# Rotary tables moved from VectorE to GpSimd, with a new order of TensorE's steps, in a hybrid decoder layer

## The chip, the cores and the metric

The kernel runs on one core of a Trainium2 chip. The metric is the device time of one execution in microseconds. The engines are called PE (TensorE), DVE (VectorE), ACT (ScalarE), POOL (GpSimd) and SP (SyncE, which issues most transfers). Times inside a profile are microseconds from the first instruction of the span.

## What is computed

One decoder layer over 256 positions of width 1024, in float32: an input projection, two groups of eight heads (A: dilated windows with a position bias, B: low-rank latents with a rotary part), an output projection with a residual, and a feed-forward block of width 4096 with squared ReLU. Cut to what matters:

```
xn = rms_norm(x, norm_mix_g)
qa, ka, va, c_q, c_kv, k_rope = split(xn @ w_in)      # 512, 512, 512, 768, 256, 32 columns
qa, ka = rms_norm per head of 64;  out_a = dilated_attention(qa, ka, va, rel_bias)
qb = rms_norm(c_q) @ w_uq;  k_nope, vb = split(rms_norm(c_kv) @ w_ukv)
qb, kb = rms_norm per head of 96 (64 plain, 32 rotary)
qb[..., 64:], kb[..., 64:] = apply_rope(..., positions)
out_b = causal softmax attention(qb, kb, vb)
h = x + concat(out_a, out_b) @ w_o
h = h + relu(rms_norm(h) @ w_ff1)^2 @ w_ff2

def apply_rope(x, positions):                 # r = 32
    ang = positions * inv_freq                # (256, 16)
    x1, x2 = x[..., :16], x[..., 16:]
    return concat([x1 * cos(ang) - x2 * sin(ang), x2 * cos(ang) + x1 * sin(ang)])
```

## The kernel before

**Tiling.** The 256 positions are two tiles of 128 partitions (`t` = 0, 1). Weights come in chunks of up to 1 MB (`raw`, three buffers, issued on SP) and are split piece by piece, 1024 columns at most, into two parts that a matmul takes exactly: ACT casts the upper part (`his`, line 243), DVE subtracts it from the weight (`los`, line 244). Each has five buffers. A step of a projection (`three`) is six matmuls: upper weights with upper and lower activations, lower weights with upper activations. Activations are split in the same way (line 276, `two`): first the columns of x, later the latents after their transposition.

**Order.** TensorE's order is written out by hand: the string `STEPS` (line 125) is read from left to right, a star gives repetitions, and every matmul is kept in that order until the feed-forward block. In it `p` is a step of q's and k's projection of group A, `b` the spread position bias, `c0`, `c1` steps of the query latents, `l` of the key latents, `g` of A's values; `A0`, `A1` transpose A's q and k; `L0` to `L2` transpose and split the latents; `x0` to `x5` are A's scores with softmax, and `y0` to `y5` the transposes of these probabilities (`keys_first`); `q0`, `q1`, `k0`, `k1` project B's queries and keys, `Q` and `K` turn them (transposes, then copies by ACT and DVE, line 636), `a` is A's probabilities times values, `s`, `t`, `v` are the same three for B, `w` steps of the output projection, `h` the residual. `r0` calls `rotary_tables()` and issues nothing on TensorE. What the other engines run is ordered by a scheduler, which fills their queues from a model of the times; each engine then works its queue off strictly in order.

**Rotary tables.** Lines 352 to 389 reduce the angle and evaluate a polynomial for sine and cosine, all on DVE, in instructions over 128x32 or 128x64 (tiles `ang`, `arg`, `sq`, `trig`); `rotary_tables()` (line 392) multiplies them by gains into `tabc` and `tabs`. The keys' tables are first read in `have_ckv` (line 588) by POOL, the queries' in `have_q` (line 646) by DVE.

**Norms of A's heads.** `normed_heads` (line 473) squares q's and k's projection on ACT, sums per head on DVE (line 454), takes the power -1/2 on POOL (lines 478 and 266, tile `s_a`, four of them: q's two tiles, then k's two), and DVE multiplies (line 481). The softmax of `probs` (line 519) is a minimum over scores on DVE (line 528), the exponential on ACT (531), and a multiplication by the reciprocal sum on DVE (534), which `keys_first` waits for.

Of the kernel before, what the change touches and what calls it, by code (L numbers as in the profile page):

```python
# [30 lines left out]
NOPE, ROPE = 64, 32  # L31
# [16 lines left out]
HR = ROPE // 2  # L48
MAGIC = 12582912.0
# [61 lines left out]
for _i, (_, _b, _n) in enumerate(CHUNKS):  # L111
# [10 lines left out]

STEPS = """p*13 b0 p*3 c0*4 A0 c0*4 r0 c1*5 A1 c1*3 l*2 L0 l*3 x0 l*2 x1 l g y0 g L1 g x2 g y1 g x3 g y2 g L2 g x4 k0 y3
    k0 x5 q0*2 y4 q0*4 k1*2 y5 q1 Q0 q1*2 K0 q1 a0 a1 q1*2 K1 s0 w s1 w*2 Q1 s2 w t0 s3 w t1 s4 t2 s5 w t3 v0 t4 w*2
    t5 w v1 w*5 h0 w*2 h1"""

WO_STEPS = [(k, b) for b in range(2) for k in range(4)]
WO_STEPS += [(4, 0), (5, 0), (4, 1), (6, 0), (7, 0), (5, 1), (6, 1), (7, 1)]  # L130
# [14 lines left out]
TWO_PI = pieces(2 * math.pi, 12, 2)
SIN = [(-1.0) ** i / math.factorial(2 * i + 1) for i in range(7)]
# [20 lines left out]
def tile_layer(ctx, tc, x, xt, cols_in, rows_in, w_all, out):  # L167
    nc = tc.nc
    V, A, G, T = nc.vector, nc.scalar, nc.gpsimd, Products(tc)

    const = ctx.enter_context(tc.tile_pool(name="const", bufs=1))
# [16 lines left out]
    def bank(pool=mm):  # L188
        return pool.tile([P, 512], F32, name=pool.name)
# [4 lines left out]
    def tiny(n, name, bufs=1):  # L194
        return small.tile([P, n], F32, name=name, bufs=bufs)
# [152 lines left out]
    load(out=rows, in_=rows_in)  # L348
    starting.clear()


    ang = [const.tile([P, NT, HR], F32, name=f"ang{i}") for i in range(4)]
    pos = const.tile([P, NT], F32, name="pos")
    V.tensor_copy(out=pos, in_=first[:, F_POS:F_POS + NT].bitcast(I32))
    a0, kh, kl, r = ang
    full = [P, NT, HR]
    inv = first[:, F_INV:F_INV + HR]
    V.tensor_tensor(out=a0, in0=pos.unsqueeze(2).broadcast_to(full), in1=inv.unsqueeze(1).broadcast_to(full), op=ALU.mult)

    def turns(out, in_, period):  # L360
        V.tensor_scalar(out=out, in0=in_, scalar1=1.0 / period, scalar2=MAGIC, op0=ALU.mult, op1=ALU.add)
        V.tensor_scalar(out=out, in0=out, scalar1=MAGIC, scalar2=None, op0=ALU.subtract)

    def less(out, in_, k, part):
        V.scalar_tensor_tensor(out=out, in0=k, scalar=-part, in1=in_, op0=ALU.mult, op1=ALU.add)

    turns(kh, a0, 2 * math.pi * 4096)
    for part in TWO_PI_HI[:3]:
        less(a0, a0, kh, part)
    less(r, a0, kh, TWO_PI_HI[3])  # L370
    turns(kl, r, 2 * math.pi)
    for k, part in ((kl, TWO_PI[0]), (kh, TWO_PI_HI[3]), (kl, TWO_PI[1]), (kh, TWO_PI_HI[4]), (kl, TWO_PI[2]), (kh, TWO_PI_HI[5])):
        less(a0, a0, k, part)
    arg = const.tile([P, NT, 2, HR], F32, name="arg")
    V.scalar_tensor_tensor(out=r, in0=a0, scalar=-1.0, in1=a0, op0=ALU.mult, op1=ALU.max)
    V.tensor_scalar(out=arg[:, :, 0, :], in0=r, scalar1=-1.0, scalar2=math.pi / 2, op0=ALU.mult, op1=ALU.add)
    V.tensor_scalar(out=r, in0=a0, scalar1=-1.0, scalar2=math.pi, op0=ALU.mult, op1=ALU.add)
    V.tensor_tensor(out=a0, in0=a0, in1=r, op=ALU.min)
    V.tensor_scalar(out=r, in0=a0, scalar1=-1.0, scalar2=-math.pi, op0=ALU.mult, op1=ALU.add)
    V.tensor_tensor(out=arg[:, :, 1, :], in0=a0, in1=r, op=ALU.max)  # L380
    af = arg.rearrange("p t c f -> p (t c f)")
    sq = const.tile([P, NT * ROPE], F32, name="sq")
    trig = const.tile([P, NT, 2, HR], F32, name="trig")
    tf = trig.rearrange("p t c f -> p (t c f)")
    V.tensor_tensor(out=sq, in0=af, in1=af, op=ALU.mult)
    V.tensor_scalar(out=tf, in0=sq, scalar1=SIN[6], scalar2=None, op0=ALU.mult)
    for c in SIN[5:0:-1]:
        V.scalar_tensor_tensor(out=tf, in0=tf, scalar=c, in1=sq, op0=ALU.add, op1=ALU.mult)
    V.scalar_tensor_tensor(out=tf, in0=tf, scalar=1.0, in1=af, op0=ALU.add, op1=ALU.mult)
    tabs = []  # L390

    def rotary_tables():
        for i in range(2):
            tab_c = const.tile([P, NT, ROPE], F32, name=f"tabc{i}")
            tab_s = const.tile([P, NT, ROPE], F32, name=f"tabs{i}")
            g1, g2 = (cols[:, C_ROPE + i * ROPE + z * HR:C_ROPE + i * ROPE + (z + 1) * HR].unsqueeze(1).broadcast_to(full) for z in range(2))
            cos, sin = trig[:, :, 0, :], trig[:, :, 1, :]
            V.tensor_tensor(out=tab_c[:, :, 0:HR], in0=cos, in1=g1, op=ALU.mult)
            V.tensor_tensor(out=tab_c[:, :, HR:], in0=cos, in1=g2, op=ALU.mult)
            V.scalar_tensor_tensor(out=tab_s[:, :, 0:HR], in0=sin, scalar=-1.0, in1=g2, op0=ALU.mult, op1=ALU.mult)  # L400
            V.tensor_tensor(out=tab_s[:, :, HR:], in0=sin, in1=g1, op=ALU.mult)
            tabs.append((tab_c, tab_s))

    def sumsq(src, dst):
        junk = sqs.tile([P, DM], mybir.dt.bfloat16, name="sqs")
        return A.activation(out=junk[:, :src.shape[1]], in_=src, func=AF.Square, accum_out=dst)  # L406
# [294 lines left out]
    for b in range(2):  # L701
# [2 lines left out]
        runs[f"k{b}"] = project_steps(f"ukv{b}", cT, KQ, KKV, lambda ps, b=b: have_kv(b, ps))  # L704
    single = {
        "A": stack_heads,
        "b": lambda i: spread_bias(),
        "r": lambda i: rotary_tables(),
        "x": begin_a,
        "y": lambda i: keys_first(UNITS[i], sb_a.pop(i), pT_a[UNITS[i][0]]),  # L710
        "L": lambda i: transposed_split([c[:, 384 * i:] for c in cn], 3 * i, 3 if i < 2 else KKV, G_C, *cT[:2]),
# [146 lines left out]
```

## Time and profile before

| | us |
|---|---|
| median of 3 runs | 322.23 (321.21 to 322.47) |
| the profiled execution | 322.39, its span 320.6 |
| PE busy | 310.5 (97%) |
| DVE busy | 219.9 (69%) |
| ACT busy | 178.4 (56%) |
| POOL busy | 40.9 (13%) |

A busy time counts the instructions of an engine in the span. A line in the profile names the source line, the engine, the operation, the tile that it writes and the tiles that it reads; `[2.00 <-DVE half L534]` says that the engine stood idle for 2.00 us before it and was released by DVE's instruction of line 534. Where a row has `x2`, two instructions of a kind are put together. The granted clock (PEclk) is TensorE's, 1.00 being 2.4 GHz.

### The profile page before, as it was taken

How to read it: one execution, taken by the hardware profiler on the slowest of the kernel's cores; microseconds unless marked ns; L12 is line 12 of the kernel's file. 1: busy time of each engine (PE TensorE's matmuls, PEld its weight loads, DVE VectorE, ACT ScalarE, POOL GpSimd, SP SyncE). 2: the span in 40 equal slices, each digit the busy share in tenths (PEclk: the TensorE clock that was granted, in tenths of full speed). 3: DMA queues.
4: the chain of work that ended last, by engine and by line, in shares of the span. 5: the costliest groups of instructions: out<-in, count | busy, mean ns of one | idle time of the engine just before them, and what ended most of it. 6: DMA issues, size and time to landing. Idle time of an engine off the chain costs nothing.

```text
span 320.6 us, 4529 instructions
## 1 busy us (share of the span) xinstructions
PE 310.5 (97%) x1646; PEld 264.9 (83%) x1646; DVE 219.9 (69%) x421; ACT 178.4 (56%) x317; POOL 40.9 (13%) x66
## 2 busy tenths in 40 slices
PE   8999999799989899999999999999999999999995
PEld 6778999587988687888888888888888888888883
DVE  3998999757868985538995584674754945845722
ACT  4885678567775684419575354543643643635400
POOL 3057501700381200000200000000000000000000
PEclk9999999799999999999999999999999999999999
DMA  7996883434342453304658455645556374553002
GB/s 226 406 372 236 288 306 140 116 101 147 133 164 66 117 214 131 133 0 138 257 193 308 164 186 200 214 181 184 212 151 241 133 234 159 190 203 131 0 35 98
DMA packets 12326, 56.95 MB, mean 178 GB/s; under 512 B 1384, under 2 KB 3440, under 8 KB 7696
## 3 DMA queue, kind: packets, MB, share of 16 engines
q1 hardware_dynamic: 10560, 54.94, 49.3%
q10 hardware_dynamic: 1744, 1.73, 1.9%
q8 instruction: 13, 0.21, 0.3%
q14 instruction: 9, 0.07, 0.1%
HBM read 55.07 MB, written 1.06 MB: 175 GB/s over the span
## 4 chain that ended last, share of the span: by engine, by line
PE 86%; DVE 7%; ACT 3%; DMA 1%; issue 1%; DVEq 0%; ACTq 0%
PE acc L160 48%; PE sc L160 20%; PE mm L160 15%; PE mm L163 4%; DVE los L244 3%; ACT his L243 2%; DMA raw<-in_weights_dram 1%; DVE half L528 1%; ACT sqs L406 1%; DVE s_q L454 0%; DVE two L276 0%; DVE half L767 0%; ACT two L275 0%; DVE nats L620 0%; ACT big L642 0%
## 5 line engine op out<-in xcount | busy, mean ns | idle before, releaser
L244 DVE TENSOR_TENSOR los<-raw,his 128x1024 fp32r<-128x1024 f32 (+3 forms) x106 | 120.9, 1148 | 61.4 <-ACT his L243 60.2
L243 ACT CAST his<-raw 128x1024 fp32r<-128x1024 f32 (+3 forms) x106 | 104.1, 990 | 87.5 <-PE acc L160 48.8
L160 PE MATMUL acc<-his,two 128*128 128x512 f32 (+2 forms) x288 | 73.9, 378 | 0.8 <-DVE two L276 0.5
L160 PE MATMUL acc<-two,his 128*128 128x512 f32 x240 | 63.1, 393 | 0.2 <-DVE half L767 0.2
L160 PEld LDWEIGHTS acc<-his,two 128*128 128x128 f32 x288 | 50.6, 190 | 8.3 <-issue 1.0
L160 PE MATMUL mm<-his,big 128*128 128x512 f32 x128 | 49.1, 390 | 0.0
L160 PE MATMUL sc<-his,big 128*128 128x512 f32 x128 | 49.0, 389 | 0.0
L160 PEld LDWEIGHTS acc<-two,his 128*128 128x128 f32 x240 | 42.6, 189 | 7.6 <-DVE half L767 0.4
L160 PE MATMUL acc<-los,two 128*128 128x512 f32 (+2 forms) x144 | 41.5, 369 | 0.0
L160 PEld LDWEIGHTS acc<-two,los 128*128 128x128 f32 x240 | 34.5, 190 | 3.4
L160 PE MATMUL acc<-two,los 128*128 128x256 f32 x240 | 35.8, 282 | 0.0
L160 PEld LDWEIGHTS acc<-los,two 128*128 128x128 f32 x144 | 26.5, 190 | 4.2 <-DVE los L244 0.6
L160 PEld LDWEIGHTS mm<-his,big 128*128 128x128 f32 x128 | 24.1, 188 | 4.8
L160 PEld LDWEIGHTS sc<-his,big 128*128 128x128 f32 x128 | 24.1, 188 | 4.8
L160 PE MATMUL sc<-los,big 128*128 128x512 f32 x64 | 24.9, 389 | 0.0
L160 PE MATMUL mm<-los,big 128*128 128x512 f32 x64 | 24.9, 389 | 0.0
L531 ACT ACTIVATE half<-half,mx 128x128 f32<-128x128 f32 (+1 forms) x32 | 14.3, 451 | 6.5 <-DVE mx L528 6.5
L766 ACT COPY half<-acc 128x256 f32<-128x256 f32 x30 | 9.8, 374 | 7.8 <-PE acc L160 7.8
L160 PEld LDWEIGHTS mm<-los,big 128*128 128x128 f32 x64 | 12.0, 188 | 2.5
L160 PEld LDWEIGHTS sc<-los,big 128*128 128x128 f32 x64 | 12.0, 188 | 2.5
L767 DVE TENSOR_TENSOR half<-acc,half 128x256 f32<-128x256 f32 x30 | 11.4, 418 | 1.3 <-ACT half L766 1.3
L770 ACT CAST big<-half 128x512 fp32r<-128x512 f32 x16 | 10.0, 625 | 3.9 <-DVE half L768 3.9
(146 smaller groups left out, 305.2 us busy)
## 6 DMA issues: line engine op xcount, KB each, us to landing
raw<-in_weights_dram SPq DMA_DIRECT2D x36, 1024.0 KB, 4.8
raw<-in_weights_dram SPq DMA_DIRECT2D x13, 512.0 KB, 5.3
raw<-in_weights_dram SPq DMA_DIRECT2D x6, 768.0 KB, 4.3
raw<-in_weights_dram SPq DMA_DIRECT2D x2, 576.0 KB, 4.6
x<-in_x_dram SPq DMA_DIRECT2D x2, 512.0 KB, 8.6
big<-vec_d ACTq DMA_DIRECT2D x1, 1024.0 KB, 6.7
big<-in_xt_dram SPq DMA_DIRECT2D x3, 256.0 KB, 6.9
raw<-in_weights_dram SPq DMA_DIRECT2D x2, 384.0 KB, 2.9
```

The costliest lines, as they stand in the source:

```text
L160: return self._issue(self.tc.nc.tensor.matmul(**kw))
L163: return self._issue(self.tc.nc.tensor.transpose(**kw))
L243: pinned(A.copy(out=hi, in_=raw))
L244: pinned(V.tensor_tensor(out=lo, in0=raw, in1=hi.bitcast(F32), op=ALU.subtract))
L406: return A.activation(out=junk[:, :src.shape[1]], in_=src, func=AF.Square, accum_out=dst)
L528: V.tensor_tensor_reduce(out=sb[:, i, :], in0=ps[:, i, :], in1=mask(h)[:, S - nk:], op0=ALU.add, op1=ALU.min, scale=scale(t, h), scalar=-L ...
L531: A.activation(out=sb[:, i, :], in_=sb[:, i, :], func=AF.Exp, scale=-1.0, bias=mx[:, i:i + 1], accum_out=mx[:, 4 + i:5 + i])
L766: A.copy(out=zs, in_=ps[2 * b + i][:, S:])
L767: V.tensor_tensor(out=zs, in0=ps[2 * b + i][:, 0:S], in1=zs, op=ALU.add)
L770: A.copy(out=ht[:, sl, :], in_=s3)
```

## The change

`rotary_tables()` now holds the whole computation, and nearly all of it is written for POOL (`G`). Where DVE had one instruction for two operations (`scalar_tensor_tensor`), POOL gets two (`two_step`), with a scratch tile `rot2` of two buffers. The cast of `pos` and three steps with a maximum or minimum stay on DVE. `r0` is called behind `A1`, no longer in front of `c1`. In `STEPS`, `L1` and `L2` stand earlier, `g` steps move between the `x` and `y`, `Q0` behind `a1`, and one `w` moves from behind `t4` to the front of `s0`.

```diff
-STEPS = """p*13 b0 p*3 c0*4 A0 c0*4 r0 c1*5 A1 c1*3 l*2 L0 l*3 x0 l*2 x1 l g y0 g L1 g x2 g y1 g x3 g y2 g L2 g x4 k0 y3
-    k0 x5 q0*2 y4 q0*4 k1*2 y5 q1 Q0 q1*2 K0 q1 a0 a1 q1*2 K1 s0 w s1 w*2 Q1 s2 w t0 s3 w t1 s4 t2 s5 w t3 v0 t4 w*2
-    t5 w v1 w*5 h0 w*2 h1"""
+STEPS = """p*13 b0 p*3 c0*4 A0 c0*4 c1*5 A1 r0 c1*3 l*2 L0 l*3 x0 l*2 L1 l x1 g*2 y0 x2 g*2 y1 g L2 x3 g*2 y2 g x4 k0 y3 k0 x5
+    q0*2 y4 q0*4 k1*2 y5 q1*3 K0 q1 a0 a1 Q0 q1*2 K1 w s0 w s1 w*2 Q1 s2 w t0 s3 w t1 s4 t2 s5 w t3 v0 t4 w t5 w v1 w*5
+    h0 w*2 h1"""
...
-    V.tensor_tensor(out=a0, in0=pos.unsqueeze(2).broadcast_to(full), in1=inv.unsqueeze(1).broadcast_to(full), op=ALU.mult)
...
-    def less(out, in_, k, part):
-        V.scalar_tensor_tensor(out=out, in0=k, scalar=-part, in1=in_, op0=ALU.mult, op1=ALU.add)
...
+    def rotary_tables():
...
+        V.tensor_copy(out=pos, in_=first[:, F_POS:F_POS + NT].bitcast(I32))
...
+        G.tensor_tensor(out=a0, in0=pos.unsqueeze(2).broadcast_to(full), in1=inv.unsqueeze(1).broadcast_to(full), op=ALU.mult)
+
+        def two_step(out, in0, scalar, in1, op0, op1):
+            tmp = tiny(NT * ROPE, "rot2", bufs=2)[:, :math.prod(in0.shape[1:])]
+            tmp = tmp.rearrange("p (t f) -> p t f", t=NT) if len(in0.shape) == 3 else tmp
+            G.tensor_scalar(out=tmp, in0=in0, scalar1=scalar, scalar2=None, op0=op0)
+            G.tensor_tensor(out=out, in0=tmp, in1=in1, op=op1)
+
+        def turns(out, in_, period):
+            G.tensor_scalar(out=out, in0=in_, scalar1=1.0 / period, scalar2=MAGIC, op0=ALU.mult, op1=ALU.add)
+            G.tensor_scalar(out=out, in0=out, scalar1=MAGIC, scalar2=None, op0=ALU.subtract)
+
+        def less(out, in_, k, part):
+            two_step(out=out, in0=k, scalar=-part, in1=in_, op0=ALU.mult, op1=ALU.add)
...
+        V.scalar_tensor_tensor(out=r, in0=a0, scalar=-1.0, in1=a0, op0=ALU.mult, op1=ALU.max)
+        G.tensor_scalar(out=arg[:, :, 0, :], in0=r, scalar1=-1.0, scalar2=math.pi / 2, op0=ALU.mult, op1=ALU.add)
+        G.tensor_scalar(out=r, in0=a0, scalar1=-1.0, scalar2=math.pi, op0=ALU.mult, op1=ALU.add)
+        V.tensor_tensor(out=a0, in0=a0, in1=r, op=ALU.min)
+        G.tensor_scalar(out=r, in0=a0, scalar1=-1.0, scalar2=-math.pi, op0=ALU.mult, op1=ALU.add)
+        V.tensor_tensor(out=arg[:, :, 1, :], in0=a0, in1=r, op=ALU.max)
...
+        for c in SIN[5:0:-1]:
+            two_step(out=tf, in0=tf, scalar=c, in1=sq, op0=ALU.add, op1=ALU.mult)
```

How it moves the queues is shown at three places. The names are those of the code, with a buffer's number where rows would read alike; a star of TensorE's steps is not printed. In the changed kernel the lines behind the tables have numbers higher by 6 (244, 266 and 276 stay).

DVE's queue at the splits of q's and k's weights, before:

```order
L276 SCALAR_TENSOR_TENSOR two<-big,first,two 128x256 x2
L365 SCALAR_TENSOR_TENSOR ang_198<-ang_199,ang_198 128x32
L244 TENSOR_TENSOR los<-raw,his 128x1024
L375 SCALAR_TENSOR_TENSOR ang_201<-ang_198 128x32
L276 SCALAR_TENSOR_TENSOR two<-big,first,two 128x256
L376 TENSOR_SCALAR arg<-ang_201 128x2x16
L244 TENSOR_TENSOR los<-raw,his 128x1024
```

and after:

```order
L276 SCALAR_TENSOR_TENSOR two<-big,first,two 128x256 x2
L398 SCALAR_TENSOR_TENSOR ang_565<-ang_562 128x32
L244 TENSOR_TENSOR los<-raw,his 128x1024
L276 SCALAR_TENSOR_TENSOR two<-big,first,two 128x256
L401 TENSOR_TENSOR ang_562<-ang_562,ang_565 128x32
L244 TENSOR_TENSOR los<-raw,his 128x1024
L403 TENSOR_TENSOR arg<-ang_562,ang_565 128x2x16
```

The rotary steps that fed each other on DVE are gone, and the three that are left read tiles that POOL writes.

POOL's queue at the norms of A's heads, before (`s_a` of q's two tiles, then of k's first):

```order
L478 TENSOR_SCALAR s_a_361<-s_a_361,eps_x 128x8
L266 TENSOR_TENSOR s_a_361<-s_a_361,mhalf 128x8
L478 TENSOR_SCALAR s_a_369<-s_a_369,eps_x 128x8
L266 TENSOR_TENSOR s_a_369<-s_a_369,mhalf 128x8
L478 TENSOR_SCALAR s_a_422<-s_a_422,eps_x 128x8
L266 TENSOR_TENSOR s_a_422<-s_a_422,mhalf 128x8
```

and after, from q's second tile to k's first (twelve steps of the tables stand at the line of dots):

```order
L484 TENSOR_SCALAR s_a_331<-s_a_331,eps_x 128x8
L380 TENSOR_SCALAR rot_626<-trig 128x64
L266 TENSOR_TENSOR s_a_331<-s_a_331,mhalf 128x8
L381 TENSOR_TENSOR trig<-rot_626,sq 128x64
...
L484 TENSOR_SCALAR s_a_384<-s_a_384,eps_x 128x8
L381 TENSOR_TENSOR tabs_641<-rot_644,cols 128x2x16
L266 TENSOR_TENSOR s_a_384<-s_a_384,mhalf 128x8
```

Fifty instructions of the tables now stand ahead of the power for k's first tile, and in the same queue as it.

TensorE's order around the first transposes of probabilities (`mm<-ident,half`), before:

```order
L160 MATMUL sc<-big,two 128x256 x4
L160 MATMUL acc<-his,two 128x288 x4
L160 MATMUL acc<-los,two 128x288 x2
L160 MATMUL acc<-his,two 128x512 x4
L160 MATMUL acc<-los,two 128x512 x2
L163 MATMUL mm<-ident,half 128x128 x4
```

and after:

```order
L163 MATMUL mm<-ident,nats 128x128 x6
L160 MATMUL acc<-his,two 128x288 x4
L160 MATMUL acc<-los,two 128x288 x2
L160 MATMUL sc<-big,two 128x256 x4
L160 MATMUL acc<-his,two 128x512 x4
L160 MATMUL acc<-los,two 128x512 x2
L160 MATMUL acc<-his,two 128x512 x4
L160 MATMUL acc<-los,two 128x512 x2
L163 MATMUL mm<-ident,half 128x128 x4
```

The six transposes of the latents (`mm<-ident,nats`) and a second step of the values (`acc`, 128x512) now come before the probabilities' transposes.

## Rows read from the trace of the kernel before

**Rows 1.** The page, busy times of the engines in the whole span

```profile
PE 310.5 (97%) x1646; PEld 264.9 (83%) x1646; DVE 219.9 (69%) x421; ACT 178.4 (56%) x317; POOL 40.9 (13%) x66
```

**Rows 2.** Waits of PE: us in total, times, longest

```profile
PE mm L163 <- DVE half L534: 2.0, 1, 2.0
PE mm L163 <- DVE nats L621: 1.3, 2, 1.0
...
PE mm L163 <- ACT big L642: 0.8, 1, 0.8
PE acc L160 <- DVE two L276: 0.5, 1, 0.5
```

**Rows 3.** Windows: length, busy time of each engine, then the granted clock

```profile
5.50:57.00 51.50, 51.50 (x282) 45.61 (x282) 48.30 (x109) 38.76 (x69) 16.51 (x20) 1.00 0.81 290
60.00:64.00 4.00, 4.00 (x17) 3.19 (x17) 2.11 (x4) 1.67 (x3) 3.64 (x12) 0.69 0.29 117
88.00:92.00 4.00, 2.96 (x20) 2.43 (x19) 4.00 (x14) 3.87 (x10) 2.44 (x3) 1.00 0.55 211
```

**Rows 4.** Timeline of POOL: start, us, instruction; last, a window as in rows 3

```profile
26.61 3.60 POOL L266 TENSOR_TENSOR s_a<-s_a,mhalf 128x8 f32<-128x8 f32 x1
...
33.49 1.64 POOL L266 TENSOR_TENSOR s_a<-s_a,mhalf 128x8 f32<-128x8 f32 x1
...
89.78 1.98 POOL L653 TENSOR_SCALAR s_q<-s_q,eps_q 128x4 f32<-128x4 f32 x1 [0.43 <-DVE s_q L454]
...
58.76:61.21 2.45, 2.15 (x7) 1.87 (x8) 2.07 (x8) 0.45 (x4) 2.12 (x10) 0.57 0.59 132
```

**Rows 5.** Timeline of DVE beside the first and the last of these

```profile
26.91 1.80 DVE L244 TENSOR_TENSOR los<-raw,his 128x768 fp32r<-128x768 f32 x2
30.25 0.69 DVE L481 TENSOR_TENSOR half<-acc,s_a 128x512 f32<-128x512 f32 x1 [1.54 <-POOL s_a L266]
...
90.00 1.21 DVE L244 TENSOR_TENSOR los<-raw,his 128x1024 fp32r<-128x1024 f32 x1
91.14 0.48 DVE L621 TENSOR_TENSOR nats<-nats,rot 128x128 f32<-128x128 f32 x2
```

**Rows 6.** Timeline of DVE, the cast of the positions and the split at 15 us

```profile
5.26 0.16 DVE L354 CAST pos<-first 128x2 f32<-128x2 int32 x1
...
15.15 1.22 DVE L244 TENSOR_TENSOR los<-raw,his 128x1024 fp32r<-128x1024 f32 x1
```

**Rows 7.** Timeline of PE, the first matmuls with the lower part of that split

```profile
17.77 0.62 PE L160 MATMUL acc<-los,two 128*128 128x512 f32 x2
```

**Rows 8.** Windows of line 244, then of line 276: length, DVE busy, count

```profile
5.00:35.50 30.50, 16.41 (x17) 1.00 0.91 339
...
5.00:35.50 30.50, 3.67 (x8) 1.00 0.91 339
```

**Rows 9.** DVE from the third `s_a` to the first probabilities: timeline, then the window

```profile
35.51 0.68 DVE L481 TENSOR_TENSOR half<-acc,s_a 128x512 f32<-128x512 f32 x1
...
58.63 0.87 DVE L534 TENSOR_SCALAR half<-half,mx 128x128 f32<-128x128 f32 x4
...
35.50:58.60 23.10, 21.56 (x143) 20.94 (x142) 22.06 (x45) 18.48 (x44) 4.64 (x9) 1.00 0.67 223
```

**Rows 10.** Timeline of PE: L1's transposes and a step of `g`, with their followers

```profile
62.49 0.82 PE L163 MATMUL mm<-ident,nats 128*128 128x128 f32 x6
63.08 1.17 PE L160 MATMUL acc<-his,two 128*128 128x512 f32 x4
...
65.00 1.09 PE L160 MATMUL acc<-his,two 128*128 128x512 f32 x4
...
66.40 0.60 PE L163 MATMUL mm<-ident,half 128*128 128x128 f32 x4
```

**Rows 11.** Timelines of DVE and of PE at t5, B's last probabilities

```profile
122.82 0.61 DVE L534 TENSOR_SCALAR half<-half,mx 128x256 f32<-128x256 f32 x2
...
124.73 0.60 PE L163 MATMUL mm<-ident,half 128*128 128x128 f32 x4
```

More of the change, by code (lines that the diff above doesn't have):

```diff
@@ L349, in tile_layer @@
     starting.clear()
[L352 to L357, printed above, removed]
-    V.tensor_tensor(out=a0, in0=pos.unsqueeze(2).broadcast_to(full), in1=inv.unsqueeze(1).broadcast_to(full), op=ALU.mult)
-    def turns(out, in_, period):
-        V.tensor_scalar(out=out, in0=in_, scalar1=1.0 / period, scalar2=MAGIC, op0=ALU.mult, op1=ALU.add)
-        V.tensor_scalar(out=out, in0=out, scalar1=MAGIC, scalar2=None, op0=ALU.subtract)
@@ L364, in less @@
-    def less(out, in_, k, part):
-        V.scalar_tensor_tensor(out=out, in0=k, scalar=-part, in1=in_, op0=ALU.mult, op1=ALU.add)
[L367 to L402, printed above, removed]
@@ L416, in tile_layer @@
     G.tensor_scalar(out=eps_x, in0=ssx, scalar1=EPS, scalar2=None, op0=ALU.mult)
+    tabs = []
+    def rotary_tables():
+        ang = [const.tile([P, NT, HR], F32, name=f"ang{i}") for i in range(4)]
+        pos = const.tile([P, NT], F32, name="pos")
+        V.tensor_copy(out=pos, in_=first[:, F_POS:F_POS + NT].bitcast(I32))
+        a0, kh, kl, r = ang
+        full = [P, NT, HR]
+        inv = first[:, F_INV:F_INV + HR]
+        G.tensor_tensor(out=a0, in0=pos.unsqueeze(2).broadcast_to(full), in1=inv.unsqueeze(1).broadcast_to(full), op=ALU.mult)
[9 more added lines that the diff above has]
+            two_step(out=out, in0=k, scalar=-part, in1=in_, op0=ALU.mult, op1=ALU.add)
+        turns(kh, a0, 2 * math.pi * 4096)
+        for part in TWO_PI_HI[:3]:
+            less(a0, a0, kh, part)
+        less(r, a0, kh, TWO_PI_HI[3])
+        turns(kl, r, 2 * math.pi)
+        for k, part in ((kl, TWO_PI[0]), (kh, TWO_PI_HI[3]), (kl, TWO_PI[1]), (kh, TWO_PI_HI[4]), (kl, TWO_PI[2]), (kh, TWO_PI_HI[5])):
+            less(a0, a0, k, part)
+        arg = const.tile([P, NT, 2, HR], F32, name="arg")
+        V.scalar_tensor_tensor(out=r, in0=a0, scalar=-1.0, in1=a0, op0=ALU.mult, op1=ALU.max)
[4 more added lines that the diff above has]
+        V.tensor_tensor(out=arg[:, :, 1, :], in0=a0, in1=r, op=ALU.max)
+        af = arg.rearrange("p t c f -> p (t c f)")
+        sq = const.tile([P, NT * ROPE], F32, name="sq")
+        trig = const.tile([P, NT, 2, HR], F32, name="trig")
+        tf = trig.rearrange("p t c f -> p (t c f)")
+        G.tensor_tensor(out=sq, in0=af, in1=af, op=ALU.mult)
+        G.tensor_scalar(out=tf, in0=sq, scalar1=SIN[6], scalar2=None, op0=ALU.mult)
+        for c in SIN[5:0:-1]:
+            two_step(out=tf, in0=tf, scalar=c, in1=sq, op0=ALU.add, op1=ALU.mult)
+        two_step(out=tf, in0=tf, scalar=1.0, in1=af, op0=ALU.add, op1=ALU.mult)
+        for i in range(2):
+            tab_c = const.tile([P, NT, ROPE], F32, name=f"tabc{i}")
+            tab_s = const.tile([P, NT, ROPE], F32, name=f"tabs{i}")
+            g1, g2 = (cols[:, C_ROPE + i * ROPE + z * HR:C_ROPE + i * ROPE + (z + 1) * HR].unsqueeze(1).broadcast_to(full) for z in range(2))
+            cos, sin = trig[:, :, 0, :], trig[:, :, 1, :]
+            G.tensor_tensor(out=tab_c[:, :, 0:HR], in0=cos, in1=g1, op=ALU.mult)
+            G.tensor_tensor(out=tab_c[:, :, HR:], in0=cos, in1=g2, op=ALU.mult)
+            two_step(out=tab_s[:, :, 0:HR], in0=sin, scalar=-1.0, in1=g2, op0=ALU.mult, op1=ALU.mult)
+            G.tensor_tensor(out=tab_s[:, :, HR:], in0=sin, in1=g1, op=ALU.mult)
+            tabs.append((tab_c, tab_s))
@@ L706, in tile_layer @@
         "A": stack_heads,
+        "r": lambda i: rotary_tables(),
         "b": lambda i: spread_bias(),
-        "r": lambda i: rotary_tables(),
         "x": begin_a,
```

## The prediction

> **What bounds the kernel now.** I read the busy shares first: TensorE works for 310.5 of the 320.6 us of the profiled span [rows 1], so any gain has to come out of time in which it stands still or runs slowly. Next I read who TensorE waits for [rows 2]: DVE's probabilities once for 2.0 us, DVE's turned q (`nats`) for 1.3 us in two waits, ScalarE's copy of turned q for 0.8, a split of the turned latents for 0.5. That is 4.6 us, and these are the places that the new order rearranges. Then the clock: in the stretch 60 to 64 us, behind the 2.0 us wait, the granted clock was 0.69, a mix of the two levels 2.4 and 1.2 GHz, which costs about (1 - 0.69) x 4 = 1.2 us; behind the wait of 1.0 us in 88 to 92 us it stayed at 1.00 [rows 3]. From 5.5 to 57 us, where the rotary chain runs on DVE, TensorE is busy for the whole 51.5 us [rows 3], so the DVE time that the chain takes isn't on the path. What the change can win is its reordering; what it can lose is the start.
>
> **Part 1, the rotary tables on GpSimd.** DVE loses 31 rows of its queue, GpSimd gets 53. The order shows three things that the diff doesn't. First, the chain isn't run beside the latents' products, where the list of steps calls it: GpSimd begins it as soon as DVE has cast `pos`, at 5.4 us [rows 6]. Second, three small steps stay on DVE, and each now waits for GpSimd in the middle of DVE's queue, the first (new L398) in front of the last four 128x1024 splits of q's and k's weights. Third, GpSimd's own small rows (`rstd`, `qk_a` and the norms of q's and k's heads, `s_a`) now stand among the chain: up to the power for the third `s_a` there are 66 rows, three of them powers over 128x8.
>
> How fast is GpSimd at this? With DVE at the probabilities beside it, it needs 0.27 us a row: in 58.76 to 61.21 us lie nine short rows, dependent ones among them, and the tail of a tenth [rows 4], 2.45 / 9. A power over 128x8 takes 1.64 [rows 4]. So 63 x 0.27 + 3 x 1.64 = 21.9 us; begun at 5.4 it would be done at 27.3, and nobody would wait for the third `s_a`, which DVE reaches at 35.51 [rows 9].
>
> But it isn't alone. The trace shows a GpSimd row that meets a DVE row with two SBUF operands: the power of 26.61 us took 3.60 instead of 1.64, and DVE's two splits run from 26.91 to 28.71; the 128x4 row of 89.78 took 1.98, and it ended 0.14 us after DVE's split and the rotary sums behind it did, at 91.62 [rows 4, 5]. DVE then waited 1.54 us for the first of these powers [rows 5]. The Trainium skill ("SBUF — State Buffer", "Who interferes with whom") says that a VectorE instruction with two SBUF inputs contends with a GpSimd instruction that reads SBUF, and that whichever starts first keeps the shared ports for the whole instruction. That speaks against this change; on the first half the trace agrees (3.60 against 1.64 us), the second half is the last rival below.
>
> Only the beginning of a power needs the way to SBUF: that of 33.49 us took its 1.64 us [rows 4] beside two splits. From 5 to 35.5 us DVE is busy for 16.41 us with 17 weight splits and for 3.67 with 8 splits of x [rows 8], each with two SBUF operands: 20.1 us. If no GpSimd row gets in between, the third `s_a` is there at 5.4 + 21.9 + 20.1 - 3 x 1.3 (the inner part of the powers) = 43.5. So the bounds of that moment, T, are 35.5 (DVE arrives then anyway) and 43.5. I take T = 42, near the upper end, because the rows that met a split sat it out, one of them across several DVE rows without a break [rows 4, 5]; 1.5 us are for those that slip in between two DVE rows.
>
> Who waits for T? DVE, with the third `s_a` ahead of everything in its queue: the lower halves of q, the latents' copies, the splits, the first probabilities. From 35.5 to 58.6 us DVE is busy for 22.06 of 23.1 us [rows 9], so a delay at 35.5 arrives at the first probabilities (multiplication of 58.63 us) nearly undiminished: **+6.5 us**.
>
> An earlier stand is covered by that one. Of the 25 GpSimd rows ahead of new L398, DVE's queue, almost without a gap up to the split of 15.15 us [rows 6], lets through some 12; the other 13 x 0.27 = 3.5, begun where DVE stops, at about 15, put L398 at 18.5 and the 1.22 us split behind it [rows 6] at 19.9, where TensorE wants it at 17.77 [rows 7]: 2 us of waiting (0 to 5.5), and perhaps 1.2 for the clock. TensorE would lose it again at the first probabilities, since these come 6.5 us later whatever it does before; it counts only if T is early.
>
> What DVE is freed from, rotary steps in the first 25 us, I count at nothing: TensorE didn't wait there [rows 3], so no wait of TensorE becomes shorter by it.
>
> **Part 2, turns of the latents and the probabilities.** Ahead of the first `y0` stand now L1 (six transposes) and a second step of `g`. They take 63.08 - 62.49 = 0.59 and 66.40 - 65.00 = 1.40 us [rows 10], together 2.0, and TensorE does them while it waited before. On DVE two splits of turned latents now stand ahead of the first probabilities' multiplication, and not behind it: 2 x 0.4 us, the price of 3.67 / 8 [rows 8], 0.8. So **-1.2 us**. The clock's 1.2 us would come back only if the wait falls to about a microsecond, as the longest for `nats`, 1.0 us, behind which it stayed at full speed [rows 2, 3]; with T at 42 the wait is longer, so I count nothing. Two `g` steps instead of one between the later `x` and `y` only add cover. L2 comes earlier, and its splits with it: the 0.5 us wait for `two` [rows 2] goes.
>
> **Part 3, turns of q.** Q0 stands behind two more q1 steps and the values a0, a1, Q1 behind one more `w`. With that the 1.3 us for `nats` and the 0.8 us for `big` [rows 2] have new cover, two q1 steps with the values and one `w` (six matmuls as wide as a `g` step's, 1.4 us), and go. Late is now t5: one `w` less between t4 and t5, and its multiplication ends at 122.82 + 0.61 = 123.4 against the transposes at 124.73 [rows 11], a reserve of 1.3: a stand of up to 0.4. The waits of parts 2 and 3 together: 0.5 + 1.3 + 0.8 - 0.3 = **-2.3 us** (bounds -2.7 and -1).
>
> **The sum.** 6.5 - 1.2 - 2.3 = +3.0 us. The profiled execution took 322.39 us for its span of 320.6, the median of the three runs is 322.23: I add to the median, **325.2 us**. With T from 39 to 43.5 and the gains from -2.2 to -3.9 the case spans 322 to 328.
>
> **Rivals.**
> (a) GpSimd gets in between DVE's rows nearly always, since DVE's rows are shorter without the rotary steps and DVE waits for ScalarE's halves now and then. Then T stays at 35.5, `s_a` are even earlier, the wait at `y0` falls to 0.8 us, and the clock stays up: -1.2 - 1.2 - 2.3 = -4.7, **317.5 us**. For it: with 27.3 us GpSimd has 8 us of reserve, and from 58.76 us on, beside DVE's work on the probabilities, nothing held it [rows 4]. Against it: the rows of 26.61 and 89.78 [rows 4].
> (b) It gets in half of the time: T about 38 to 39, +3, with the same gains: **322 us**, no change.
> (c) GpSimd holds DVE up as well, when its row is first: then nothing overlaps, the inner part of the powers neither, T = 5.4 + 21.9 + 20.1 = 47.4, +11.9 - 3.5 = **330.6 us**. This is the second half of the skill's sentence above. Against it: the splits beside the power of 26.61 took 1.80 for two [rows 5], as elsewhere. It decides only from T over 43.5.
> (d) The step list's gains don't come, with T early: a new wait at t5, or a bank for L1 that isn't free, takes 2 us of the 4.7: 319.5 us.
>
> **How the numbers follow.** A difference under 0.5% (1.6 us) can't be told from none. The forecast has a chance of 0.47; nearly all of it lies above 323.8. Rival (a) with (d) has 0.29, all of it faster; (b) 0.16, nearly all of it within 0.5%; (c) 0.08. Slower: 0.44 + 0.08 = 0.52 with a bit of (b) taken off, 0.50; faster 0.31; same 0.19. The range leaves out (c) and the better end of (a): 316.8 to 328.0. Since cases of both signs are in it, the likeliest one's own range is 322 to 328.
>
> **What would show it.** Right: GpSimd's rows of the chain last 0.4 us and more on average between 5 and 35 us, not 0.27; DVE waits for GpSimd at new L398 for over 2 us and at the multiplications by `s_a` (new L487), the third of them ending its wait near 42; TensorE waits for a split near 18 us and for the first probabilities for 2 us or more, at about 65; no wait for q's turns. Wrong: DVE reaches the third `s_a` at about 36 without a wait, the chain's rows take 0.27 us, and the wait at `y0` is under a microsecond at full clock: then it is (a), and the step that failed is that a DVE row keeps GpSimd out.

## The result: slower by 0.9%, and the profile after

The changed kernel takes 324.74 us (median of 5 runs, 323.94 to 325.68) against 322.23 (5 runs, 321.21 to 322.69). The ratio is 1.0087 with a 95% interval of 1.0058 to 1.0115. The profiled execution has a span of 322.9 us, that of before 320.6. The lines of the program stand 6 lower than before (`half` L481 is now L487, L534 is L540). Every profile below is of an execution within 0.5 us of its kernel's median.

The page's busy times, to be held against [rows 1]: DVE lost 34 rows and 3.9 us, GpSimd got 52 rows and 21.6 us (the prediction had counted 31 and 53 rows; all 52, not fifty, stand ahead of the power for the third `s_a`). 52 rows at the 0.27 us that the prediction read off would be 14.0.

```profile
PE 311.2 (96%) x1646; PEld 266.1 (82%) x1646; DVE 216.0 (67%) x387; ACT 177.7 (55%) x317; POOL 62.5 (19%) x118
```

Who PE waits for (us in total, times, longest), against [rows 2]: nothing of the old list is left except the first probabilities, 1.4 instead of 2.0. The waits for turned q, for its copy and for turned latents are gone. In their place stand four waits that the kernel before didn't have, all ahead of the first probabilities: at 18.52 us for a split (1.0), at 33.48 for a split (0.9), at 36.63 for q's first multiplied half (1.1) and at 48.91 for `two` (2.2).

```profile
PE mm L163 <- DVE two L501: 2.2, 1, 2.2
PE mm L163 <- DVE half L540: 1.4, 1, 1.4
...
PE mm L163 <- DVE half L487: 1.1, 1, 1.1
PE acc L160 <- DVE los L244: 1.0, 1, 1.0
PE sc L160 <- DVE los L244: 0.9, 1, 0.9
```

DVE is late there because it waits for GpSimd, and GpSimd is late because its rows are long. First DVE's waits, then single rows of GpSimd's timeline (start, us, instruction), then DVE's beside them.

```profile
DVE half L487 <- POOL s_a L266: 9.5, 3, 5.0
...
DVE ang L398 <- POOL ang L381: 2.6, 1, 2.6
```

```profile
17.41 1.13 POOL L399 TENSOR_SCALAR arg<-ang 128x32 f32<-128x32 f32 x1 [0.32 <-DVE ang L398]
...
25.62 1.50 POOL L380 TENSOR_SCALAR rot<-trig 128x64 f32<-128x64 f32 x1
...
27.94 0.38 POOL L380 TENSOR_SCALAR rot<-trig 128x64 f32<-128x64 f32 x1
...
38.13 1.00 POOL L380 TENSOR_SCALAR rot<-trig 128x32 f32<-128x32 f32 x1
39.10 0.25 POOL L421 TENSOR_TENSOR tabs<-trig,cols 128x32 f32<-128x32 f32 x1
...
39.52 1.03 POOL L419 TENSOR_TENSOR tabc<-trig,cols 128x32 f32<-128x32 f32 x1
40.52 1.00 POOL L380 TENSOR_SCALAR rot<-trig 128x32 f32<-128x32 f32 x1
...
42.62 1.67 POOL L266 TENSOR_TENSOR s_a<-s_a,mhalf 128x8 f32<-128x8 f32 x1
```

```profile
17.24 1.22 DVE L244 TENSOR_TENSOR los<-raw,his 128x1024 fp32r<-128x1024 f32 x1
...
25.95 0.93 DVE L244 TENSOR_TENSOR los<-raw,his 128x768 fp32r<-128x768 f32 x1
31.87 0.69 DVE L487 TENSOR_TENSOR half<-acc,s_a 128x512 f32<-128x512 f32 x1 [4.98 <-POOL s_a L266]
...
37.95 1.02 DVE L244 TENSOR_TENSOR los<-raw,his 128x768 fp32r<-128x768 f32 x1
38.90 0.67 DVE L460 TENSOR_REDUCE s_a<-sqs 128x8 f32<-128x512 f32 x1
39.49 1.87 DVE L244 TENSOR_TENSOR los<-raw,his 128x768 fp32r<-128x768 f32 x2
44.32 0.69 DVE L487 TENSOR_TENSOR half<-acc,s_a 128x512 f32<-128x512 f32 x1 [2.96 <-POOL s_a L266]
...
67.68 0.87 DVE L540 TENSOR_SCALAR half<-half,mx 128x128 f32<-128x128 f32 x4
```

Read them side by side. The row of 17.41 takes 1.13 us, and a split of DVE runs from 17.24 to 18.46. The row of 25.62 takes 1.50 us, with a split from 25.95 to 26.88; a row of the same line and size at 27.94 takes 0.38, while DVE itself stands still, from 26.89 to 31.87. Between 37.95 and 41.36 DVE runs three splits of 128x768 and, between the first and the second, a reduction with one operand. The three rows of GpSimd that meet a split take 1.00 to 1.03; the one of 39.10, beside the reduction, takes 0.25. It and the row of 39.52 multiply the same sizes. DVE gets the third `s_a` at 44.32 instead of 35.51 [rows 9], and starts the multiplication of the first probabilities at 67.68 instead of 58.63.

The clock, in windows as in [rows 3] (length, PE busy, granted clock): full speed behind the 1.4 us wait at 68 us, but a mix of the two levels behind the 2.2 us wait at 48.91. These two stretches cost (1 - 0.72) x 4 + (1 - 0.85) x 4 = 1.7 us in this execution.

```profile
48.00:52.00 4.00, 3.05 (x14) 0.72 0.91 293
52.00:56.00 4.00, 4.00 (x24) 0.85 0.83 289
...
68.00:72.00 4.00, 3.88 (x20) 1.00 0.38 131
```

### The profile page after: what moved, and what is told of

Same layout as the page of the kernel before. It is cut to its first block, busy times and chain, and to the rows that moved or that the text cites. A ratio compares the mean times of both kernels' runs of the same rounds, so it can differ in the third digit from the quotient of the medians.

```text
span 322.9 us, 4547 instructions
## 1 busy us (share of the span) xinstructions
PE 311.2 (96%) x1646; PEld 266.1 (82%) x1646; DVE 216.0 (67%) x387; ACT 177.7 (55%) x317; POOL 62.5 (19%) x118
## 4 chain that ended last, share of the span: by engine, by line
PE 76%; POOL 11%; DVE 4%; ACT 3%; issue 2%; DMA 1%; DVEq 0%; ACTq 0%; POOLq 0%
PE acc L160 40%; PE sc L160 17%; PE mm L160 14%; PE mm L163 4%; POOL rot L380 3%; POOL s_a L266 2%; ACT his L243 2%; DVE los L244 2%; DMA first<-in_xt_dram 1%; POOL ang L381 1%; ACT sqs L353 1%; POOL trig L381 1%; DVE two L276 1%; ACT two L275 1%; POOL rstd L266 1%
## 5 line engine op out<-in xcount | busy, mean ns | idle before, releaser
L244 DVE TENSOR_TENSOR los<-raw,his 128x1024 fp32r<-128x1024 f32 (+3 forms) x106 | 121.4, 1153 | 60.4 <-ACT his L243 60.3
L160 PEld LDWEIGHTS acc<-his,two 128*128 128x128 f32 x288 | 51.5, 192 | 6.6 <-issue 0.8
L163 PE MATMUL mm<-ident,half 128*128 128x128 f32 x64 | 10.5, 286 | 4.7 <-DVE two L501 2.2
L163 PEld LDWEIGHTS mm<-ident,half 128*128 128x128 f32 x64 | 7.9, 142 | 7.6 <-issue 4.4
```

The lines of the kernel that those rows point to most:

```text
L160: return self._issue(self.tc.nc.tensor.matmul(**kw))
L163: return self._issue(self.tc.nc.tensor.transpose(**kw))
L244: pinned(V.tensor_tensor(out=lo, in0=raw, in1=hi.bitcast(F32), op=ALU.subtract))
```

## The experiments

My theory after the result: the list of steps gains what its parts promise; the tables on GpSimd cost more than that, since the chain's rows read SBUF, are held while DVE runs its splits, and stand ahead of `s_a`, for which DVE and then everything behind it wait. Rivals: the order itself loses; the number of rows in GpSimd's queue is what counts, not the hold; the three handoffs between GpSimd and DVE are the cause; GpSimd holds DVE as well; the early wait at 18 us is what counts.

### The two halves of the change, each alone

The new list of steps with the tables left on DVE (the kernel before, with `STEPS` of the changed one):

```diff
-STEPS = """... c0*4 r0 c1*5 A1 c1*3 ... (before)
+STEPS = """... c0*4 c1*5 A1 r0 c1*3 ... (changed)
```

> The new list of steps alone; the rotary tables stay on DVE, where they were before. My theory (the order gains, the tables on GpSimd lose): no wait of TensorE for turned q, turned latents or its copy, the wait for the first probabilities falls from 2.0 to about 0.8 us and the clock behind it stays at 1.00; the third power for s_a ends near 35.5 us as before; 4 to 5 us faster than before, 317 to 318.5 us. Rival (the order itself loses, the tables on GpSimd win something): no better than before, 322 us or more, with the first probabilities late although the third s_a is early.

Measured: 316.41 us against 321.57 for the kernel before, run beside it, ratio 0.9837 (0.9818 to 0.9856). Of PE's waits behind the start, one over half a microsecond is left (the expectation had 317 us as its lower end):

```profile
PE mm L163 <- DVE half L534: 0.8, 1, 0.8
```

The tables on GpSimd with the old list of steps (the changed kernel, with `STEPS` of before):

> The tables on GpSimd alone, with the list of steps of before. My theory: DVE gets the third s_a near 44 us as in the changed kernel (44.3) instead of 35.5; TensorE waits for the first probabilities for over 5 us, and the 0.5, 1.3 and 0.8 us waits for turned latents and turned q stay; 6.5 to 8.5 us slower than before, 328.5 to 331 us. Rival (the order is what loses): about as before, 321.5 to 323 us.

Measured: 330.70 us, ratio 1.0280 (1.0257 to 1.0302). DVE gets the third `s_a` at 44.29 us, 0.03 from the changed kernel, and TensorE's waits for the first probabilities and for turned q are both there (waits of PE):

```profile
PE mm L163 <- DVE half L540: 3.2, 1, 3.2
PE mm L163 <- DVE two L501: 2.2, 1, 2.2
PE mm L163 <- DVE nats L627: 1.3, 2, 1.0
```

The wait at the probabilities is 3.2 and not over 5 us: PE had lost the rest earlier, 2.2 of it at `two`. So the change is two changes of opposite sign, -5.2 and +9.1 us (330.70 - 321.57). The rival that the order loses is out. In the new order the tables cost a little less: 324.74 - 316.41 = 8.3 us.

The list of steps in its two parts, tables on DVE: the first run (e6) has the new half up to `x5`, the second (e7) the new half from `q0` on.

> Tables on DVE as before; of the list of steps only the first half is new (turns of the latents and probabilities). My theory: 1.2 us of waiting at the first probabilities, 1.2 of the clock behind it and 0.5 for turned latents go, the 1.3 and 0.8 us for turned q stay: 2.9 us faster than before, 318.3 to 319.3 us. Rival (a wait ahead of the q part only moves on to it): 320.5 us or more.

> Tables on DVE as before; of the list of steps only the second half is new (turns of q, values, the probabilities t5). My theory: the 1.3 and 0.8 us waits for turned q go, no new one of over 0.4 us at t5; the 2.0 us wait at the first probabilities and the clock of 0.69 behind it stay: 1.8 to 2.2 us faster than before, 319.3 to 320 us. Rival (a new wait at t5 takes part of it): 320.8 us or more.

Measured, against 322.13 for the kernel before: 318.98 us, ratio 0.9903 (0.9884 to 0.9922), for the latents and probabilities; 319.68, ratio 0.9926 (0.9899 to 0.9953), for q. They add up to -5.6, the two together had -5.2. Neither wait comes back elsewhere, and none appears at t5.

### Does the chain's place do it, and is DVE's freed time worth anything?

The whole chain on GpSimd, its three DVE steps too, queued behind the last power for `s_a`:

```diff
-        "r": lambda i: rotary_tables(),
+        "r": lambda i: tables_behind_norms(),
...
+    def tables_behind_norms():
+        with tc.issue_after(last_norm[0]):
+            rotary_tables()
...
-        V.tensor_tensor(out=a0, in0=a0, in1=r, op=ALU.min)
+        G.tensor_tensor(out=a0, in0=a0, in1=ramp(a0, 2.0, -math.pi), op=ALU.subtract)
```

> The changed kernel, but the whole chain of the tables (its three DVE steps too, written as ramps that GpSimd can do) stands in GpSimd's queue behind the last power for s_a. My theory (the loss comes from the chain standing ahead of the small rows of s_a and of the three handoffs with DVE): no wait of DVE at the first table step nor at the products with s_a, third power for s_a done by 36 us, tables ready well before DVE turns k; 317 to 318.5 us, as with the tables on DVE. If time freed on DVE is worth something, it beats that run by 1 us or more. Rival (GpSimd's rows slow DVE down wherever they stand): DVE's splits and probabilities between 36 and 65 us take longer and the time stays at 320.5 us or more.

Measured: 316.80 us, ratio 0.9843 (0.9825 to 0.9861). The third power for `s_a` is done at 33.89, and the chain follows it (timelines of GpSimd, then of DVE):

```profile
32.25 1.64 POOL L266 TENSOR_TENSOR s_a<-s_a,mhalf 128x8 f32<-128x8 f32 x1
...
35.95 0.24 POOL L375 TENSOR_TENSOR ang<-pos,first 128x32 f32<-128x32 f32 x1
...
50.75 1.16 POOL L412 TENSOR_TENSOR sq<-arg 128x64 f32<-128x64 f32 x1
...
63.98 0.22 POOL L628 TENSOR_TENSOR rot<-kr,tabs 128x16 f32<-128x16 f32 x1
```

```profile
33.92 0.69 DVE L491 TENSOR_TENSOR half<-acc,s_a 128x512 f32<-128x512 f32 x1 [0.44 <-POOL s_a L266]
```

The chain now begins at 35.95, and its first user, the keys' rotary part on GpSimd, follows right behind it at 63.98, 6.8 us later than the 57.17 of the kernel before. Rows are held here too (1.16 us at 50.75), but neither DVE nor PE waits for the tables. The same work on the same engine costs 8 us in one place of the queue and nothing that these runs can tell from none in the other. It also gains nothing: 316.80 (316.42 to 317.05) with the tables on GpSimd, 316.41 (316.18 to 316.95) with the tables on DVE. The time that DVE is freed from is worth nothing to this kernel.

### The hold or the number of rows?

The chain's rows on GpSimd replaced by about as many fills that read nothing from SBUF, in the same places, with the same three DVE steps between (51 fills, and at the handoffs four copies of 128x2, which do read); constants stand for the tables:

```diff
-        less(a0, a0, k, part)
...
+        def fill(t, n):
+            for _ in range(n):
+                G.memset(t, 0.5)
...
+        fill(angle, 25)
```

> The changed kernel with the chain's rows on GpSimd replaced by as many fills of 128x200 that read nothing, in the same place of the queue and with the same three DVE steps waiting for them; leaves out the computation of the tables, which hold constants. My theory (GpSimd's rows that read SBUF are held while DVE runs a row with two SBUF operands; fills aren't): the fills take 0.2 to 0.35 us each beside DVE's splits too, the wait at the first of the three DVE steps is under 0.5 us, the third power for s_a is done before 37 us, 317 to 319 us. Rival (it is the mere number of rows ahead, at a slower rate per row early on): third s_a near 44 us and 324 to 325 us as the changed kernel.

Measured: 318.38 us, ratio 0.9895 (0.9879 to 0.9912). The fills, as groups of rows of GpSimd (busy, mean ns):

```profile
L375 POOL MEMSET ang<- 128x200 f32 x26 | 6.9, 267 | 1.5
...
L375 POOL MEMSET tab<- 128x200 f32 x25 | 6.6, 266 | 1.2
```

51 fills take 267 ns each on average (260 to 272), beside the same splits of DVE: none is held. Some rows between them that do read SBUF still are: two of the copies take 1.12 us, two small rows 0.9 and 1.2. The chain's own rows in the changed kernel take 0.23 to 0.40 when they aren't held, so the fills don't win by being much shorter. The handoffs and the queue remain, and the third `s_a` comes at:

```profile
37.47 0.69 DVE L456 TENSOR_TENSOR half<-acc,s_a 128x512 f32<-128x512 f32 x1 [1.54 <-POOL s_a L266]
```

That is 6.9 us earlier than in the changed kernel, and the time is 6.4 us lower. So the hold of the chain's rows is most of the loss. My expectation had missed the rest by a little (before 37 us): the third `s_a` is still 3.3 us later than the 34.20 at which DVE takes it with the tables on DVE, and the time 2.0 us above that run. The handoffs, the number of rows ahead and the other rows that are held are worth about a quarter together; these two runs don't take them apart.

Half of it: only the 24 rows behind the three DVE steps as one copy and 23 fills. Here, too, constants stand for the tables.

```diff
-        G.tensor_tensor(out=sq, in0=af, in1=af, op=ALU.mult)
...
+        G.tensor_copy(out=table[:, 0:2], in_=arg[:, 0, 1, 0:2])
+        for _ in range(23):
+            G.memset(table, 0.5)
```

> The changed kernel; of the chain on GpSimd the 24 rows behind the three DVE steps are replaced by one copy of 128x2 and 23 fills of 128x200 that read nothing; leaves out the sines and the tables, which hold constants. First part, handoffs and small rows stay. My theory (rows of the second part that read SBUF are held by DVE's splits, also by those behind 35.5 us): the third s_a comes 4 to 6 us earlier than 44.3, at 38 to 40 us, and TensorE loses about as much less: 319 to 321 us, between the run with all rows as fills (37.4 us, 318.4) and the changed kernel. Rival (the first part and the handoffs set the third s_a): within 1.5 us of 44.3 and 323.5 us or more.

Measured: 321.14 us, ratio 0.9981 (0.9965 to 0.9996) to 321.31. DVE still waits for the first of the three steps (3.3 us, 2.6 in the changed kernel), and takes the third `s_a` at 40.27; this and the time lie just outside what was expected:

```profile
40.27 0.69 DVE L474 TENSOR_TENSOR half<-acc,s_a 128x512 f32<-128x512 f32 x1 [0.44 <-POOL s_a L266]
```

Of the 6.9 us of hold, 4.0 belong to the second part of the chain, and 2.8 to the first, as far as two runs with other waits of DVE can be subtracted.

### The handoffs and the early wait

The three DVE steps on GpSimd as well, the chain early as in the changed kernel (the second `-`/`+` pair of the diff above, without `issue_after`):

> The changed kernel with the three table steps that had stayed on DVE moved to GpSimd too (a maximum and a minimum written as ramps, six more rows there); the chain still starts early and stands ahead of the small rows of s_a. My theory (the hold of GpSimd's rows by DVE's splits sets the third s_a, the handoffs only the stand at 17 to 18 us, which the later one covers): the 2.6 us wait of DVE at the first table step and the 1.0 us wait of TensorE at 18.5 us go; the third s_a stays within 2 us of 44.3, and the time within 1.6 us of the changed kernel's 324.7. Rival (the three handoffs are the cause): the third s_a before 39 us and 319 us or less.

Measured: 325.78 us, ratio 1.0114 (1.0092 to 1.0135). The stand at 18 us is gone, the third `s_a` comes at 44.19, the total is as bad, so the handoffs aren't the cause. Its executions had a mean granted clock of 0.989 to 0.994, those of the changed kernel 0.995 to 1.000, which may be the 1.0 us that it took longer. What the expectation didn't have is how (waits of PE, then of DVE, then DVE's timeline):

```profile
PE sc L160 <- DVE los L244: 4.3, 1, 4.3
```

```profile
DVE half L491 <- POOL s_a L266: 10.9, 3, 8.4
```

```profile
34.68 0.69 DVE L491 TENSOR_TENSOR half<-acc,s_a 128x512 f32<-128x512 f32 x1 [8.39 <-POOL s_a L266]
```

With no stand early on, DVE runs further ahead and then stands 8.4 us for the first `s_a`. Between 26.3 and 34.7 us, while DVE stands, no row of the chain takes over 0.4 us, so GpSimd catches up: a DVE that waits doesn't hold.

The early wait alone: the first part of the chain and the three steps as in the changed kernel, everything from the square on behind the last power for `s_a`.

```diff
+        with tc.issue_after(last_norm[0]):
             sq = const.tile([P, NT * ROPE], F32, name="sq")
```

> The changed kernel, but the part of the chain behind the three DVE steps (from the square on) stands behind the last power for s_a; the first part and the three steps stay where they are. It has the early stand alone. My theory: DVE waits 2.6 us at the first table step and TensorE about 1.0 us at 18.5 us as in the changed kernel, the third s_a is done by 36 us; once the later delay is gone the early one counts: 317 to 318.5 us, 0.5 to 2 us above the run with the whole chain late (316.8). Rival (the early stand costs nothing, DVE makes it up before the first probabilities): 316.3 to 316.9 us; rival (the early stand sets the third s_a): 321 us or more.

Measured: 318.14 us, ratio 0.9872 (0.9851 to 0.9893). DVE waits 3.3 us at the first step and TensorE 1.2 us for the split (waits):

```profile
DVE ang L398 <- POOL ang L381: 3.3, 1, 3.3
```

```profile
PE acc L160 <- DVE los L244: 1.2, 1, 1.2
```

It is 1.3 us above the run with the whole chain late, and PE lost 1.2: with the later delay gone, the early one counts in full (317.45 to 318.18 against 316.42 to 317.05 us, not taken side by side). In the changed kernel it is covered.

### One step further

The waits of the run of the order alone left 0.77 us at the first probabilities. One more step of `g` ahead of them, taken from between x3 and y2:

```diff
-    ... l x1 g*2 y0 x2 g*2 y1 g L2 x3 g*2 y2 g x4 ...
+    ... l x1 g*3 y0 x2 g*2 y1 g L2 x3 g y2 g x4 ...
```

> The new list of steps with the tables on DVE (the run of the order alone, 316.4 us), and one more step of g ahead of the first probabilities, taken from between x3 and y2. A step of g took 1.40 us of TensorE, the wait at the first probabilities that was left was 0.77 us. My theory: that wait goes, none comes back at y2, 0.5 to 0.8 us faster than the order alone: 315.6 to 316 us. Rival (the bank of the third g is not free, or y2 now waits): 316.4 us or more.

Measured: 315.56 us, ratio 0.9810 (0.9786 to 0.9834) to 321.31; from 32 to 72 us PE has no idle time left. It is the best version here, with the tables on DVE: 9.2 us below the changed kernel, 5.8 below the one before. (The order alone, taken at another time, was 316.18 to 316.95 us, this run 315.10 to 315.67.)

### All of them on one line

Third `s_a` taken by DVE, start of the transposes of the first probabilities on PE (all with the new order), and the time, in us:

| run | third `s_a` | PE at y0 | median |
|---|---|---|---|
| order alone, tables on DVE | 34.20 | 59.56 | 316.41 |
| chain late | 33.92 | 60.39 | 316.80 |
| second part late | 35.77 | 61.54 | 318.14 |
| all fills | 37.47 | 61.94 | 318.38 |
| second part fills | 40.27 | 64.75 | 321.14 |
| changed kernel | 44.32 | 68.11 | 324.74 |
| no handoffs | 44.19 | 68.65 | 325.78 |

The ends of the range, as rows (DVE and PE of the order alone, then PE of the changed kernel, whose DVE row is shown above):

```profile
34.20 0.68 DVE L481 TENSOR_TENSOR half<-acc,s_a 128x512 f32<-128x512 f32 x1
59.56 0.83 PE L163 MATMUL mm<-ident,half 128*128 128x128 f32 x4 [0.77 <-DVE half L534]
```

```profile
68.11 0.82 PE L163 MATMUL mm<-ident,half 128*128 128x128 f32 x4 [1.35 <-DVE half L540]
```

The time follows y0: 8.55 us from the first row to the changed kernel, and 8.33 in the time. From 37.47 to 44.32 it follows `s_a` at (324.74 - 318.38) / (44.32 - 37.47) = 0.93 us each; the run without handoffs lies 1 us above that.

## Why the prediction was right, and which of its terms weren't

The forecast was 325.2 us and the measurement 324.74; its mechanism, the late `s_a` behind rows that DVE holds, is shown by the fills (6.4 us come back when the rows read nothing) and by the chain moved behind `s_a` (8 us come back). Its terms were less good than their sum; that the forecast came within 0.5 us is in part luck.

**The hold, T = 42, +6.5 us.** The step is right, its sizes aren't: T was 44.32, and the tables cost 8.3 us in this order. Against the 34.20 at which DVE takes the third `s_a` in the new order with the tables on DVE, not the 35.5 of the kernel before, the delay was 10.1 us. And behind T stand two errors that cancel: the sum had 27.3 without a hold and so 14.7 for the hold; with fills in the chain's place the third `s_a` came at 37.47, so that the hold of the chain's rows took 6.9 us, and all the rest 10.2 more than was summed. (Added up row by row, 15 rows of the chain over 0.5 us stand some 10 us above their usual length; with fills, other rows are held in part instead.) The prediction counted DVE's splits up to 35.5 us, where DVE had taken the third `s_a` before, and gave 43.5 as the upper end. But a DVE that is late runs its splits later, too, and they go on holding. Between 35.5 and 44.3 the changed kernel has four rows held to 0.94 to 1.03 us, some 0.7 each beyond their 0.25 to 0.31, or 2.9 us together. I had closed the sum at a time that the sum itself moves.

**27.3 us if nothing is held.** Too early, and it carried rival (a). With unheld fills the third `s_a` still came at 37.47. Fills of 0.27 us follow each other at 0.32 (timeline of GpSimd, 25 fills in 8.04 us), and in the same queue stand the handoffs, the held copies and small rows, and a fourth power, `rstd`, of 1.50 us, which the 21.9 us counted as a short row.

```profile
5.88 8.04 POOL L375 MEMSET ang<- 128x200 f32 x25
```

Rival (a), 317.5, was therefore too low: with the chain's rows never held, the fills show 318.4.

**"Arrives nearly undiminished."** Right for DVE (+8.8 us at the third `s_a`, +9.05 at the multiplication, of which 0.8 is the two splits moved ahead). Wrong in where TensorE pays: not in one wait at y0, but 0.9 and 1.1 at 33 and 37 us, 2.2 at `two`, and 1.4 at y0. Of the signs, the long rows came (0.49 us on average for the chain's 39 rows from 5 to 35 us), the wait of 2 us or more at y0 didn't.

**The clock's 1.2 us, counted as not coming back.** In the profiled execution it did come back: the wait at y0 fell to 1.4 and the clock stayed at 1.00. It was lost in another place, 1.7 us behind the wait for `two`. The price was read too low as well: [rows 4] has 0.57 from 58.76 on, ahead of the window from 60 us, and so has the stretch from 59 to 63 us, (1 - 0.57) x 4 = 1.7 us. So the two profiled executions lost the same to the clock, in different places, and this is a second part of why the total was met. It isn't settled by one execution: another of the changed kernel had a mean of 1.000 and took 325.03 us.

**The early stand, covered.** Right: DVE waited 2.6 us (L398 at 17.13, predicted 18.5), TensorE 1.0 (predicted 2), and removing it (no handoffs, with six more rows on GpSimd) didn't lower the total, while with the later delay gone it cost its 1.2.

**DVE's freed time, nothing.** Right, by 316.80 against 316.41.

**Parts 2 and 3, -1.2 and -2.3.** Right in kind: all named waits went, and the wait at the first probabilities fell from 2.0 to 0.77 in the run of the order alone, the 1.2 that was worked out. (The working has a slip: 3.67 / 8 is 0.46, so two splits are 0.9 and the term -1.1.) Q's half gave -2.45 (interval of the ratio: -1.5 to -3.3) against -1.8. The stand at t5 that I took off, 0.3, isn't there. The order alone gave -5.2, and -3.5 was counted. Of the difference some 0.7 may be the clock, by the last section; 0.3 is the stand at t5. The other 0.7 us I can't place.

**Rival (c), GpSimd holds DVE too.** Out. The Trainium skill ("SBUF — State Buffer", "SBUF: two separate sides") has the engine that starts first keep the ports for its whole instruction, and the other blocked. By that rule a GpSimd row of 0.25 us that is first could cost DVE up to that. Here DVE's splits stayed at 1.22 to 1.23 us for 128x1024 beside the chain, as in [rows 6], and went from 0.95 to at most 1.02 for 128x768, from 0.68 to at most 0.75 for 128x512; all 106 of them, of which 17 stand beside the chain, took 121.4 us with the chain on GpSimd and 120.9 without (groups of rows, busy us; the changed kernel, then the one before):

```profile
L244 DVE TENSOR_TENSOR los<-raw,his 128x1024 fp32r<-128x1024 f32 (+3 forms) x106 | 121.4, 1153 | 60.4 <-ACT his L243 60.3
```

```profile
L244 DVE TENSOR_TENSOR los<-raw,his 128x1024 fp32r<-128x1024 f32 (+3 forms) x106 | 120.9, 1148 | 61.4 <-ACT his L243 60.2
```

So the splits lost 0.5 us together and at most 0.07 each, while rows of GpSimd lost up to 1.1. Who was first can't be read from the recorded starts: the row of 25.62 and the power of 26.61 [rows 4] begin before the split beside them, and it was they that were held. That the rows on GpSimd are short may be why DVE pays so little; no run here put long rows there.

## What to carry to other kernels

Before work goes to an idle engine, list what already stands in that engine's queue and who waits for it: the chain ahead of the powers for `s_a` cost 8 us here, the same chain behind them nothing that could be told from none. A chain of short GpSimd rows that read SBUF, beside DVE rows with two SBUF operands, loses about the DVE row's length where it meets one, over the whole stretch that the delay itself lengthens. The sum of those DVE rows is an upper bound: here 20.1 us of them were counted, and 6.9 us came back when the chain read nothing. The queue without the hold, in turn, was summed 10.2 us too short: its powers, handoffs and other rows belong in the sum. And when a change has two halves, measure each: here one half was worth -5 us, and the other ate it.

## What the runs showed of the hardware

Fills that write 128x200 to SBUF and read nothing weren't held at all (267 ns on average of 51), in the stretch where rows of a sixth of that size that read took up to 1.2 us. The expectation of that run had it so.

What I had not expected is that the clock behind a wait of 2.0 us isn't settled by the wait. The kernel before and the run with q's new order have the same wait at the same place, 2.00 us in both (PE's timeline, before and then e7). Before, the matmuls behind it took 2.06 and 1.02 us at a granted clock of 0.69 [rows 3]; in e7 the same ones took 1.18 and 0.62 at 1.00.

```profile
59.06 1.07 PE L163 MATMUL mm<-ident,half 128*128 128x128 f32 x4 [2.00 <-DVE half L534]
59.79 2.06 PE L160 MATMUL acc<-his,two 128*128 128x512 f32 x4
61.64 1.02 PE L160 MATMUL acc<-los,two 128*128 128x512 f32 x2
```

```profile
59.56 0.83 PE L161 MATMUL mm<-ident,half 128*128 128x128 f32 x4 [2.00 <-DVE half L532]
60.15 1.18 PE L158 MATMUL acc<-his,two 128*128 128x512 f32 x4
61.16 0.62 PE L158 MATMUL acc<-los,two 128*128 128x512 f32 x2
```

It differs from execution to execution of one kernel, too. Of the six executions of e7, three had a mean granted clock of 1.000 (318.8 to 319.4 us) and three 0.995 (320.0 to 320.7). Of the 37 executions of the kernel before that were taken beside the experiments, 13 had a mean granted clock of 0.999 or 1.000 and took 320.7 to 321.4 us; 17 had 0.995 or less and took 322.1 to 323.0. Their means lie 1.4 us apart. Only the profiled execution shows where its clock fell; if it fell there in the others, too, saving this wait is worth between nothing and 1.4 us of clock on top, on average 0.7 or so, an estimate (17 of 37, times 1.4). With the wait at 0.77 us (order alone, and e6) no execution had less than 0.998.
